# Output stage of a hybrid convolution/attention block on one core: VectorE's order pinned with the additions first, the convolution product's results written over its loaded operands, the last weight splits on GpSimd

## The chip, the cores and the metric

The kernel runs on one core of one Trainium2 chip. The core has five engines with instruction streams of their own: TensorE (PE, and PEld for its weight loads), VectorE (DVE), ScalarE (ACT), GpSimd (POOL) and SyncE (SP), which here issues nearly all DMA transfers. An engine works through its stream in order; where an instruction waits for another engine or for a transfer, all that stands behind it on that engine waits as well. The metric is the device time of one execution in microseconds; the time before is the median of three runs.

## What is computed

One decoder layer over a sequence of 2048 tokens with model width 1024, all in float32 (the reference, cut to the part that matters here):

```python
h = rms_norm(x, norm_w) * (1 + scale) + shift
a, b, g_conv, q, k, v, g_attn, m_conv, m_attn = split(h @ w_in)
...                                   # convolution branch -> u, attention branch -> o
y_conv = u @ w_conv_out               # (2048 x 1024) @ (1024 x 1024)
y_attn = o @ w_attn_out
y = sigmoid(m_conv) * y_conv + sigmoid(m_attn) * y_attn
out = y @ w_out
x = x + gate * out
```

The change lies in the last three lines: the product `u @ w_conv_out` with the merge behind it, and the output product `y @ w_out` with the residual addition.

## The kernel before

Every float32 operand of a matmul is split into a high part h (a copy to the reduced format fp32r, on ScalarE) and a low part l = source - h (a subtraction of 128x512 on VectorE or GpSimd), and a product is the sum of three matmuls per 128 rows: h·h, h·l, l·h. TensorE's order is the program's order (a manual schedule). The order on the other engines is chosen when the kernel is built, by the scheduler of the framework with a model of time, except for instructions handed to `tc.keep_in_program_order`, which stay in the program's order among themselves.

*The convolution product* (L1451 to L1484) has four token blocks t of 512 tokens and in each eight blocks dm of 128 output columns, "yc t_dm". Each takes 24 matmuls. For each, SP loads two 256 KB tiles: the gate `gt` (the trace calls it mc, L1474; pool `gp`, three buffers) and the finished attention part `ya` (the trace: yl, L1476; pool `ys`, tag "yt", four buffers). When the product is in PSUM, VectorE makes `yt = (gt + 1) * pz` (L1482) and `yt = yt + ya` (L1483), where `yt` is another tile of tag "yt", and SP stores it to the scratch array `y_d` in HBM (L1484). So a block takes two of the four buffers of "yt".

*The weights of the output product.* During the last token block (t = 3) `w_out` is loaded in four pieces, `wo_fetch` (L1367): `wo_raw0`, and `wo_raw1` to `wo_raw3` in pool `op` under the tag "raw" with four buffers. They are multiplied by the adaLN gate (`wo_scale`, L1375). GpSimd forms combinations in place (L1400), and `wo_split` (ScalarE L1390, then `eng` at L1391) splits them into the operands of the product: B11, B21, T1, T3, T2 during the last blocks, B22 and T4 (called through `wo_rest`, L1403) from the output stage's hooks. Each name has four pieces k = 0 to 3.

*The output stage* works in eight quads j, each of 2 x 128 tokens by 2 x 512 columns, with a Strassen-Winograd scheme of seven products instead of eight. The products are A11·B11, A12·B21, S2·T2, S1·T1, S3·T3, S4·B22, A22·T4 with the numbers 0 to 6, where A are quarters of y, S their combinations, B quarters of the scaled weights and T their combinations. They run in the order `WO_ORDER = (0, 3, 2, 1, 4, 5, 6)` of product() (L1498), which is called with product numbers 0, 3, 2, 1, 4, 5, 6 in the quad as well; each has 12 matmuls of 128x512 (L1504). There are three PSUM banks: pa (the trace: oa), pb (ob), pc (oc). The first, third, fifth and seventh product accumulate in pa one on the other, the fourth goes to pb, the second and sixth to pc. After every product VectorE adds the bank to an x tile (L1491); a product that goes on accumulating in a bank can start only when the addition of the bank's last state has read it.

For a quad, `y_load` (L1409) reads the quarters of y from `y_d` into a tile `yq{j}` (two transfers of 512 KB; tag "raw", the same four buffers as wo_raw1 to wo_raw3), `y_split` (L1416) forms one S where needed (GpSimd, L1422 to L1427, in place but for S1, "ys") and splits the operand (ScalarE yh L1431, VectorE yl L1432). The splits run five products ahead (`LEAD`). `x_load` (L1444) loads four x tiles per quad; for the even quads from 2 on, and two tiles of quad 0, they are of tag "yt". The results are stored at L1496. Note that the trace uses "yl" both for the loaded attention part (L1476) and for the low part of a y operand (L1432).

*The hooks* (`out_hooks`) place the rest: in quad 0, after the first two products, the B22 splits (L1536 and after; even k on VectorE, odd k on GpSimd), after the third to sixth the T4 splits (all on VectorE); in each quad after the first product the y load of the next quad, after the fourth its x loads, and after each product the y split five products on. A hook is called inside product(), so in the program it stands ahead of that product's addition.

Of the kernel before, what the change touches and what calls it, by code (L numbers as in the profile page):

```python
# [10 lines left out]
F32 = mybir.dt.float32  # L11
# [4 lines left out]
ALU = mybir.AluOpType  # L16
AX = mybir.AxisListType

P = 128
# [35 lines left out]
def tile_hybrid_block(  # L55
# [5 lines left out]
    nc = tc.nc  # L61
# [3 lines left out]
    def pool(name, bufs=1, **kw):  # L65
        return tc.tile_pool(name=name, bufs=bufs, reuse_waits="tile", **kw)
# [8 lines left out]
    def bank(tag, name):  # L75
        return psum.tile([P, 512], F32, tag=tag, name=name)
# [9 lines left out]
    y_d = dram.tile([KC, P, S], F32, name="y_d")  # L86
# [33 lines left out]
    with pool("start", side="right") as st:  # L120
# [34 lines left out]
        n = tab[:, :, 1, :]  # L155
# [340 lines left out]
    def merge_z(half, j, wts, hooks):  # L496
        pz = bank("z" if half == 0 and j < 4 else "zzss"[j % 4], f"pzg{half}_{j}")
        z_tokens(pz, 256, *wts, j, hooks)
        return pz
# [80 lines left out]
    def spread_load(load):  # L580
        box = []
        return {16: [lambda: box.append(load())], 23: [lambda: box.pop()()]}
# [118 lines left out]
    for i in range(8):  # L701
        half, k = divmod(i, 4)
# [22 lines left out]
    for g in GROUPS:  # L725
        for h in range(NH):
            u = NH * GROUPS.index(g) + h
            state = {}
            for j in range(NB):
# [14 lines left out]
                if u == 0 and j >= NB - 2:  # L744
                    rest = []
                    for i in range(4):
                        f = loads[4 * (j - NB + 2) + i]
# [19 lines left out]
                i = NB * (u - 2 * NH) + j - 2  # L767
# [19 lines left out]
    for j in range(3):  # L787
        hooks = {}
# [4 lines left out]
        pz = merge_z(0, j, cur, hooks)  # L793
# [50 lines left out]
    for step, (half, j) in enumerate(order):  # L844
# [11 lines left out]
        hooks = spread_load(loads[step - 4]) if 4 <= step < 4 + KC else {}  # L856
        while len(turns) >= 2:
            hooks.setdefault(3, []).append(turns.pop(0))
        pz = merge_z(half, j, wts[half], hooks)
# [302 lines left out]
    for at, (i, n) in enumerate(slots):  # L1162
# [23 lines left out]
        for name, k in asked[:2]:  # L1186
            own, tag = (gp, "gt") if k < 3 else (cv, "ld")
# [21 lines left out]
    def right(name):  # L1209
        c = tc.tile_pool(name=name, bufs=1, side="right", reuse_waits="tile")  # L1210
        return c, c.__enter__()
# [5 lines left out]
    ys = big["raw"] = ys_c.__enter__()  # L1217
# [82 lines left out]
    def at_block(n, m, f):  # L1300
        plan.setdefault(n, {}).setdefault(m, []).append(f)
# [33 lines left out]
    for t in range(NT):  # L1335
        tsl = slice(512 * t, 512 * t + 512)
        for dm in range(KC):
            gt = gp.tile([P, 512], F32, tag="gt", name=f"ma{t}_{dm}")
            nc.sync.dma_start(gt, ma_d[dm, :, tsl])
            pz = bank("zso"[dm % 3], f"ya{t}_{dm}")  # L1340
# [3 lines left out]
            yt = ys.tile([P, 512], F32, tag="yt", name=f"yt{t}_{dm}", bufs=4)  # L1344
# [14 lines left out]
    WO_ORDER = (0, 3, 2, 1, 4, 5, 6)  # L1359
# [26 lines left out]
    def wo_split(name, k, src, eng=nc.vector):  # L1386
        if name not in wo:
            wo[name] = wo_place(name)
        h, l = (x[k] if isinstance(x, list) else x[:, k] for x in wo[name])
        nc.scalar.activation(h, src, AF.Copy)  # L1390
        eng.tensor_tensor(l, src, h.bitcast(F32), op=ALU.subtract)  # L1391

    def wo_first(k):
        w = wo_raw[k]
# [8 lines left out]
    def wo_rest(name, k, eng=nc.vector):  # L1403
        h, c = {"T3": (0, 0), "T2": (0, 1), "T4": (1, 0), "B22": (1, 1)}[name]
        wo_split(name, k, wo_raw[k][:, h, c], eng)

    LEAD = 5
# [8 lines left out]
    def y_split(j, i):  # L1416
        a11, a12, a21, a22 = (ysrc[j][:, q].rearrange("p k t -> p (k t)") for q in range(4))
        pool_tt = nc.gpsimd.tensor_tensor
        n = WO_ORDER[i]
        if n == 0:  # L1420
            s1 = ysrc[j, "S1"] = ys.tile([P, 512], F32, tag="fraw", name=f"ys1_{j}", bufs=3)
            pool_tt(s1, a21, a22, op=ALU.add)  # L1422
            pool_tt(a21, a11, a21, op=ALU.subtract)
        if n == 2:
            pool_tt(a11, ysrc[j, "S1"], a11, op=ALU.subtract)
        if n == 4:
            pool_tt(a12, a12, a11, op=ALU.subtract)  # L1427
        src = (a11, a12, a11, ysrc[j, "S1"], a21, a12, a22)[n]
        own, tag, bufs = (op, "y", 2) if (j, i) in ((0, 0), (0, 1)) else (up[1], "u", KC)
        h, l = ya_of[j, n] = [own.tile([P, 512], F32R, tag=tag + hl, name=f"y{hl}{j}_{n}", bufs=bufs) for hl in "hl"]  # L1430
        nc.scalar.activation(h, src, AF.Copy)  # L1431
        nc.vector.tensor_tensor(l, src, h.bitcast(F32), op=ALU.subtract)  # L1432

    ysrc, ya_of, xin = {}, {}, {}

# [15 lines left out]
    for t in range(NT):  # L1451
        tsl = slice(512 * t, 512 * t + 512)
        if t == NT - 1:
            lnp_c.__exit__(None, None, None)
            wop_c, wop = right("wop")
            ap_c.__exit__(None, None, None)
            up_c[1].__exit__(None, None, None)
            op_c = pool("op", bufs=2)
            op = op_c.__enter__()
            for k in range(1, 4):  # L1460
                at_block(KC * t, 2, lambda k=k: wo_fetch(k))
                at_block(KC * t + (1, 2, 3)[k - 1], 1, lambda k=k: wo_scale(k))
            for k in range(4):
                at_block(KC * t + (0, 1, 2, 4)[k], (3, 6, 15, 3)[k], lambda k=k: wo_first(k))
            for i, (name, k) in enumerate((b, k) for b in ("T2", "T3") for k in range(4)):
                at_block(KC * t + 4 + i // 2, 4 + 11 * (i % 2), lambda name=name, k=k: wo_rest(name, k))
            at_block(KC * t + 4, 8, lambda: y_load(0))
            for i in range(2):
                at_block(KC * t + 6, 6 + 6 * i, lambda i=i: y_split(0, i))
            for q in (0, 3):  # L1470
                at_block(KC * t + 5, 8, lambda q=q: x_load(0, q))
        for dm in range(KC):
            gt = gp.tile([P, 512], F32, tag="gt", name=f"mc{t}_{dm}")
            nc.sync.dma_start(gt, mc_d[dm, :, tsl])  # L1474
            ya = ys.tile([P, 512], F32, tag="yt", name=f"yl{t}_{dm}", bufs=4)
            nc.sync.dma_start(ya, ya_d[dm, :, tsl])  # L1476
            pz = bank("zso"[dm % 3], f"yc{t}_{dm}")
            sl = slice(P * (dm % 4), P * (dm % 4) + P)
            project(pz, [h[:, sl] for h, _ in wc[dm // 4]], [l[:, sl] for _, l in wc[dm // 4]],
                    norms[t].uh, norms[t].ul, plan.get(KC * t + dm))  # L1480
            yt = ys.tile([P, 512], F32, tag="yt", name=f"yc{t}_{dm}", bufs=4)
            nc.vector.scalar_tensor_tensor(yt, gt, 1.0, pz, op0=ALU.add, op1=ALU.mult)  # L1482
            nc.vector.tensor_add(yt, yt, ya)  # L1483
            nc.sync.dma_start(y_d[dm, :, tsl], yt)  # L1484

    HB = NB // 2

    def out_quad(j, hooks):
        pa, pb, pc = bank("z", f"oa{j}"), bank("s", f"ob{j}"), bank("o", f"oc{j}")
        x11, x12, x21, x22 = (xin.pop((j, q)) for q in range(4))  # L1490
        add = lambda dst, ps: nc.vector.tensor_tensor(dst, dst, ps, op=ALU.add)  # L1491
        begun = set()

        def store(q, t):
            jj, c = j + HB * (q // 2), q % 2
            nc.sync.dma_start(out2[P * jj : P * jj + P, 512 * c : 512 * c + 512], t)  # L1496

        def product(n, ps, more=False):  # L1498
            yh, yl = ya_of.pop((j, n))
            wh, wl = ([x[k] if isinstance(x, list) else x[:, k] for k in range(4)] for x in wo[PRODUCTS[n][1]])  # L1500
            yh, yl = ([y[:, P * k : P * k + P] for k in range(4)] for y in (yh, yl))
            terms = [t for k in range(4) for t in ((yh[k], wh[k]), (yh[k], wl[k]), (yl[k], wh[k]))]
            for m, (y, w) in enumerate(terms):
                nc.tensor.matmul(ps, y, w, start=(m == 0 and ps.name not in begun), stop=(m == 11 and not more),  # L1504
                                 skip_group_check=True)
            begun.add(ps.name)
            hooks(WO_ORDER.index(n))

        product(0, pa, True)
        add(x11, pa)  # L1510
        product(3, pc, True)
        add(x22, pc)
        product(2, pa, True)
        add(x12, pa)
        product(1, pb)
        add(x11, pb)
        store(0, x11)
        product(4, pa, True)
        add(x22, pa)
        store(3, x22)  # L1520
        product(5, pc)
        add(x12, pc)
        store(1, x12)
        product(6, pa)
        add(x21, pa)
        store(2, x21)

    for q in (1, 2):
        x_load(0, q)
# [3 lines left out]
    def out_hooks(j):  # L1533
        def f(i):
            if j == 0 and i < 2:
                for k in (2 * i, 2 * i + 1):  # L1536
                    wo_rest("B22", k, (nc.vector, nc.gpsimd)[k % 2])
            elif j == 0 and i < 6:
                wo_rest("T4", i - 2)
            if j + 1 < HB and i == 0:  # L1540
                y_load(j + 1)
            if j + 1 < HB and i == 3:
                for q in range(4):
                    x_load(j + 1, q)
            at = 7 * j + i + LEAD
            if at < 7 * HB:
                y_split(at // 7, at % 7)
        return f
# [38 lines left out]
```

## Time and profile before

| | |
|---|---|
| median of 3 runs | 2425.87 us |
| lowest, highest run | 2423.82, 2425.93 us |
| the profiled execution: its own time | 2423.63 us |
| its span, first to last instruction | 2421.7 us |
| mean granted TensorE clock | 0.994 |
| first matmul of the output stage | 2249.9 us |
| last addition of the output stage | 2418.0 us |

All times inside the profile count from the span's start. A line of a timeline gives start and duration in us, the engine, the source line, the operation, the tiles written and read, their shapes and how many instructions were put together (x3); in brackets stands the engine's idle time before it and what ended that. A line of a view of waits gives who waited for whom, the total in us, how often, and the longest. "SPq" rows are transfers that SP issues; their duration is that of the issuing, not of the transfer.

### The profile page before, as it was taken

To read this page: it belongs to the slowest core of one execution; us is meant where nothing else is said; L and a number is where in the kernel's file an instruction comes from. 1 tells how busy PE (TensorE), PEld (TensorE's weight loads), DVE (VectorE), ACT (ScalarE), POOL (GpSimd) and SP (SyncE) were. 2 spreads that over 40 slices of the span, in tenths; PEclk is the share of its full clock that TensorE was granted. 3 is DMA by queue.
4 is the path that set the end of the run, shared out by engine and by line. 5 is a ranking of instruction groups with operands and counts; after the bars stand their busy time and mean duration, and the time that the engine had idled before them with its cause. 6 is when DMAs were issued, how large, how long until landed. Compare 5 with 4: busy or idle time off the path is not lost. (4 is left out here: it accounts for less than half of the span.)

```text
span 2421.7 us, 39474 instructions
## 1 busy us (share of the span) xinstructions
PE 2372.0 (98%) x12785; PEld 2117.9 (87%) x12785; DVE 1734.9 (72%) x3941; ACT 998.0 (41%) x2790; POOL 839.7 (35%) x949
## 2 busy tenths in 40 slices
PE   6999999999999999999999999999999999999899
PEld 2989999999999999999888888878888888888687
DVE  5865655555555565567779999989999977787643
ACT  4833433343343444344544444554444444431221
POOL 3421111111111111112467777775565620004420
PEclk8999999999999999999999999999999999999999
DMA  7633543454453222115664544674444469865742
GB/s 256 219 115 110 158 128 102 142 150 140 145 154 89 70 67 61 31 49 176 211 207 138 164 154 133 211 231 125 136 150 132 156 221 315 285 198 185 215 145 83
DMA packets 349468, 372.99 MB, mean 154 GB/s; under 512 B 29704, under 2 KB 251176, under 8 KB 349262
## 3 DMA queue, kind: packets, MB, share of 16 engines
q1 hardware_dynamic: 335966, 346.80, 46.1%
q10 hardware_dynamic: 13296, 23.66, 2.7%
q8 instruction: 102, 1.67, 0.3%
q14 instruction: 104, 0.85, 0.1%
HBM read 231.74 MB, written 138.61 MB: 153 GB/s over the span
## 5 line engine op out<-in xcount | busy, mean ns | idle before, releaser
L370 PE MATMUL pz<-wh_u,hT_lo 128*128 128x384 f32 x1536 | 537.1, 350 | 5.2 <-DVE hT_lo L289 3.8
L370 PE MATMUL pz<-wh_u,hT_hi 128*128 128x384 f32 x1536 | 518.3, 337 | 5.3 <-ACT wh_u L346 2.9
L370 PE MATMUL pz<-wl_u,hT_hi 128*128 128x384 f32 x1536 | 518.9, 338 | 0.6 <-DVE wl_u L349 0.6
L398 DVE SCALAR_TENSOR_TENSOR qk<-pz,st,wqk 128x128 f32<-128x128 f32 x384 | 117.0, 346 | 318.3 <-POOL st L114 318.1
L113 POOL TENSOR_SCALAR st<-st 128x2 f32<-128x2 f32 x192 | 47.3, 247 | 812.7 <-ACT sq L387 812.7
L370 PEld LDWEIGHTS pz<-wh_u,hT_hi 128*128 128x128 f32 x1536 | 290.7, 189 | 8.2 <-ACT wh_u L346 3.6
L370 PEld LDWEIGHTS pz<-wh_u,hT_lo 128*128 128x128 f32 x1536 | 289.4, 188 | 8.1 <-DVE hT_lo L289 4.6
L370 PEld LDWEIGHTS pz<-wl_u,hT_hi 128*128 128x128 f32 x1536 | 289.8, 189 | 2.0 <-DVE wl_u L349 1.5
L434 ACT ACTIVATE qkT<-ptq 128x256 f32<-128x256 f32 x192 | 73.6, 383 | 420.2 <-PE ptq L432 419.7
L1033 DVE SCALAR_TENSOR_TENSOR ce<-us,pair_taps,ce 128x512 f32<-128x512 f32 x240 | 179.8, 749 | 1.7
L1004 DVE SCALAR_TENSOR_TENSOR ce<-ut,chan,ce 128x512 f32<-128x512 f32 x240 | 179.5, 748 | 0.0
L1017 DVE SCALAR_TENSOR_TENSOR cq<-ut,chan,cq 128x512 f32<-128x512 f32 x208 | 156.5, 752 | 4.2
L919 POOL TENSOR_TENSOR slT<-wT,shT 128x512 fp32r<-128x512 f32 x97 | 129.4, 1336 | 75.3 <-ACT shT L918 75.3
L387 ACT ACTIVATE sq<-pz 128x128 bf16<-128x128 f32 x384 | 106.0, 276 | 99.6 <-PE pz L370 92.6
L114 POOL TENSOR_TENSOR st<-st,mhalf 128x2 f32<-128x2 f32 x192 | 136.6, 712 | 16.0
L918 ACT ACTIVATE shB<-wB 128x512 fp32r<-128x512 f32 x120 | 75.5, 631 | 152.0 <-issue 44.5
L918 ACT ACTIVATE shT<-wT 128x512 fp32r<-128x512 f32 x100 | 63.1, 631 | 153.0 <-issue 66.2
L919 POOL TENSOR_TENSOR slB<-wB,shB 128x512 fp32r<-128x512 f32 x77 | 102.4, 1330 | 68.5 <-ACT shB L918 67.1
L447 ACT ACTIVATE sm<-sm,osb 128x128 f32<-128x128 f32 (+1 forms) x192 | 88.7, 462 | 62.6 <-DVE osb L445 59.6
L461 PE MATMUL po<-lv,pT 128*128 128x128 f32 x600 | 97.2, 273 | 0.0
L461 PEld LDWEIGHTS po<-lv,pT 128*128 128x128 f32 x600 | 93.0, 189 | 0.5 <-issue 0.5
L445 DVE CUSTOM_DVE_ANT_0 sm<-ps,mask 128x128 f32<-128x128 f32 (+1 forms) x192 | 68.7, 358 | 26.5 <-PE ps L442 26.4
(666 smaller groups left out, 6331.5 us busy)
## 6 DMA issues: line engine op xcount, KB each, us to landing
wB<-in_w_in_dram SPq DMA_DIRECT2D x140, 256.0 KB, 3.3
qkv_d<-qkv SPq DMA_DIRECT2D x128, 192.0 KB, 2.2
wT<-tT_d SPq DMA_DIRECT2D x80, 256.0 KB, 2.7
raw_u<-in_w_in_dram SPq DMA_DIRECT2D x93, 192.0 KB, 2.8
lqk<-qkv_d SPq DMA_DIRECT2D x128, 128.0 KB, 2.3
tT_d<-wB ACTq DMA_DIRECT2D x60, 256.0 KB, 2.8
acc_d<-osb SPq DMA_DIRECT2D x192, 65.0 KB, 1.8
at<-acc_d SPq DMA_DIRECT2D x64, 195.0 KB, 3.5
```

What stands on the lines that cost most here:

```text
L114: nc.gpsimd.tensor_tensor(dst, scratch[:, :n], mhalf[:, :n], op=ALU.pow)
L370: nc.tensor.matmul(pz[:, :width], part(a, k, P * j, P), w[:, :width], start=(m == 0), stop=(m == 23))
L387: nc.scalar.activation(sq, pz[:, P * i : P * i + P], AF.Square, scale=1.0 / math.sqrt(P), accum_out=st[:, i : i + 1])
L398: nc.vector.scalar_tensor_tensor(qk[:, 2 * i : 2 * i + 2].rearrange("p a b -> p (a b)"), pz[:, P * i : P * i + P], st[:, 2 + i : 3 + i], w ...
L434: nc.scalar.activation(qkT.rearrange("p a b -> p (a b)"), pt[:, :256], AF.Copy)
L447: nc.scalar.activation(sm[:, :w], sm[:, :w], AF.Exp, scale=-1.0, bias=o[:, P : P + 1], accum_out=o[:, P + 1 : P + 2])
L461: nc.tensor.matmul(po[:, :P], box["pT"][:, P * i : P * i + P], vt, start=(i == 0), stop=(i == nk - 1))
L918: nc.scalar.activation(h, q[name], AF.Copy)
L919: eng.tensor_tensor(l, q[name], h.bitcast(F32), op=ALU.subtract)
L1004: stt(box["e"], e[:, 1 + j : 513 + j], chan[:, cb, 2 * j : 2 * j + 1], box["e"], op0=ALU.mult, op1=ALU.add)
L1017: stt(box["o"], o[:, 2 + j : 514 + j], w, psum_o, op0=ALU.mult, op1=ALU.add)
L1033: stt(dst, box["both"][:, 1 + j : 513 + j], pair_taps[:, cb, j : j + 1], box["e"], op0=ALU.mult, op1=ALU.subtract if j == 0 else ALU.add)
```

## The change

1. *Order pinned on VectorE.* Three kinds of instruction are kept in program order among themselves: the additions of the output stage, the y splits from quad 0's sixth product on, and the T4 splits on VectorE. And the hooks are called behind the addition of their product, not ahead of it.
2. *Results over the operands.* The convolution product's first VectorE operation writes over the gate tile, the second over the loaded attention part, which is then stored. A block so takes one buffer of "yt", not two, and the ya load of a block takes the buffer that the store of four blocks earlier has read. The gate tile comes free after the second operation instead of the first.
3. *Late splits on GpSimd.* All four B22 splits and the T4 splits k = 1 and 3 run on GpSimd; T4 k = 0 and 2 stay on VectorE. Four subtractions move in all.

```diff
@@ wo_split
-        eng.tensor_tensor(l, src, h.bitcast(F32), op=ALU.subtract)
+        ins = eng.tensor_tensor(l, src, h.bitcast(F32), op=ALU.subtract)
+        if name == "T4" and eng is nc.vector:
+            tc.keep_in_program_order(ins)
@@ y_split
-        nc.vector.tensor_tensor(l, src, h.bitcast(F32), op=ALU.subtract)
+        ins = nc.vector.tensor_tensor(l, src, h.bitcast(F32), op=ALU.subtract)
+        if (j, i) >= (0, LEAD):
+            tc.keep_in_program_order(ins)
@@ convolution product
-            yt = ys.tile([P, 512], F32, tag="yt", name=f"yc{t}_{dm}", bufs=4)
-            nc.vector.scalar_tensor_tensor(yt, gt, 1.0, pz, op0=ALU.add, op1=ALU.mult)
-            nc.vector.tensor_add(yt, yt, ya)
-            nc.sync.dma_start(y_d[dm, :, tsl], yt)
+            nc.vector.scalar_tensor_tensor(gt, gt, 1.0, pz, op0=ALU.add, op1=ALU.mult)
+            nc.vector.tensor_add(ya, ya, gt)
+            nc.sync.dma_start(y_d[dm, :, tsl], ya)
@@ out_quad
-        add = lambda dst, ps: nc.vector.tensor_tensor(dst, dst, ps, op=ALU.add)
+        add = lambda dst, ps: tc.keep_in_program_order(nc.vector.tensor_tensor(dst, dst, ps, op=ALU.add))
...
             begun.add(ps.name)
-            hooks(WO_ORDER.index(n))
 
         product(0, pa, True)
         add(x11, pa)
+        hooks(0)
         product(3, pc, True)
         add(x22, pc)
+        hooks(1)
...
         product(6, pa)
         add(x21, pa)
         store(2, x21)
+        hooks(6)
@@ out_hooks
             if j == 0 and i < 2:
                 for k in (2 * i, 2 * i + 1):
-                    wo_rest("B22", k, (nc.vector, nc.gpsimd)[k % 2])
+                    wo_rest("B22", k, nc.gpsimd)
             elif j == 0 and i < 6:
-                wo_rest("T4", i - 2)
+                wo_rest("T4", i - 2, (nc.vector, nc.gpsimd)[i % 2])
```

More of the change, by code (lines that the diff above doesn't have):

```diff
@@ L1506, in product @@
             begun.add(ps.name)
-            hooks(WO_ORDER.index(n))
         product(0, pa, True)
         add(x11, pa)
+        hooks(0)
         product(3, pc, True)
         add(x22, pc)
+        hooks(1)
         product(2, pa, True)
         add(x12, pa)
+        hooks(2)
         product(1, pb)
@@ L1517, in out_quad @@
         store(0, x11)
+        hooks(3)
         product(4, pa, True)
@@ L1520, in out_quad @@
         store(3, x22)
+        hooks(4)
         product(5, pc)
@@ L1523, in out_quad @@
         store(1, x12)
+        hooks(5)
         product(6, pa)
```

## The prediction

> **What bounds the kernel now.** I read the page first (busy shares), then TensorE's waits over the last 320 us, then the chain of waits and the engines' timelines around the one wait that is left there.
>
> ```profile
> span 2421.7 us, 39474 instructions
> PE 2372.0 (98%) x12785; PEld 2117.9 (87%) x12785; DVE 1734.9 (72%) x3941; ACT 998.0 (41%) x2790; POOL 839.7 (35%) x949
> ```
> ```profile
> PE oa L1504 <- DVE xt L1491: 8.9, 1, 8.9
> ```
> TensorE is busy 98% of the span, and in the stages that the change touches it waits for long once only: 8.9 us, for an addition of the first output quad. The chain that ended last shows where:
>
> ```profile
> 2261.99 1.81 DVE woloT L1391 x3
> 2263.79 0.61 DVE xt L1491
> 2264.40 0.14 issue
> 2264.53 5.21 PE oa L1504 x12
> 2269.74 2.81 PE ob L1504 x12
> 2272.55 2.80 PE oa L1504 x12
> 2275.35 2.80 PE oc L1504 x12
> 2278.15 5.60 PE oa L1504 x24
> ```
> ```profile
> 2249.90 0.40 PE L1504 MATMUL oa<-wohB,yh 128*128 128x512 f32 x1
> ```
> The first product of the quad starts at 2249.90 and a product takes 2.80, so the third is due at 2255.50. It accumulates in the bank of the first (pa) and starts at 2264.53, when the addition that reads that bank is done. It then takes 5.21 instead of 2.80. The seventh product starts at 2278.15; undisturbed it would at 2255.50 + 4 x 2.80 = 2266.7. The place costs 11.4 us (0.47%), which is all that the change can win here. Windows (columns: PE, PEld, DVE, ACT, POOL busy, granted clock, DMA share, GB/s) explain the 5.21:
>
> ```profile
> 2255.60:2259.10 3.50, 0.01 (x1) 0.00 (x0) 3.50 (x4) 2.19 (x5) 3.50 (x3) 1.00 0.55 153
> 2259.10:2264.50 5.40, 0.00 (x0) 0.00 (x0) 5.40 (x10) 1.04 (x3) 1.13 (x1) 0.50 0.29 80
> 2264.50:2269.30 4.80, 4.76 (x11) 3.80 (x12) 1.78 (x3) 1.00 (x2) 1.60 (x2) 0.50 1.12 335
> ```
> The clock falls to 0.50 some 3.5 us into the idle time and is still there for 4.8 us of work after it: 5.21 - 2.80 = 2.4 us. VectorE was busy all through the gap, with other things:
>
> ```profile
> 2250.90 0.69 DVE L1483 TENSOR_TENSOR yc<-yc,yl 128x512 f32<-128x512 f32 x1 [2.82 <-DMA yl<-ya_d]
> 2253.87 1.89 DVE L1432 TENSOR_TENSOR yl<-yq,yh 128x512 fp32r<-128x512 f32 x3
> 2255.68 3.43 DVE L1391 TENSOR_TENSOR woloB<-wo_raw,wohiB 128x512 fp32r<-128x512 f32 x2
> 2259.62 1.76 DVE L1432 TENSOR_TENSOR yl<-yq,yh 128x512 fp32r<-128x512 f32 x2
> 2261.91 1.88 DVE L1391 TENSOR_TENSOR woloT<-wo_raw,wohiT 128x512 fp32r<-128x512 f32 x3
> 2263.72 0.67 DVE L1491 TENSOR_TENSOR xt<-xt,oa 128x512 f32<-128x512 f32 x1
> ```
>
> **The additions first.** In the new built order the first addition follows the last convolution block's two operations directly; the two B22 splits (3.43), the three T4 splits (1.88) and two of the y splits (1.76) no longer stand ahead of it. What is then last is the load of the last block's gate operand, mc: by the sum below it issues about 2250.7, and the ya loads of the same size land 2.9 to 4.8 us after issue (second landing row below), which gives 2253.6 to 2255.5; two block operations and the addition, 0.69 + 0.69 + 0.67, and the 0.14 of the chain put the third product at 2255.8 to 2257.7, 0.3 to 2.2 us late, less than the 3.5 after which the clock fell. So the old stall goes.
>
> **What the pins put in its place.** After three additions and T4's first split, the pinned order on VectorE is: y split of quad 1 for its first product; addition of quad 0's fourth product (bank pb); y split of quad 1 for its second product; addition of quad 0's fifth product (bank pa). The seventh product writes pa and so waits for that last one. Both splits need yq1, quad 1's y. Before, those additions were not held by yq1. So the question is when yq1 is loaded, and there two of the other parts come in. (1) Its buffer: the rotation of four gives it wo_raw1's, whose last reader is now T4's split k=1 on GpSimd. (2) Its place in SP's queue: writing results over the loaded operands means that a ya load four blocks on, and four x loads, take a buffer that a store still reads, so each waits for a store's landing, and SP issues nothing meanwhile. In the new SP order come: store 3_3, mc, ya 3_7 (waits for store 3_3), store 3_4, mc 3_7, x (waits for 3_4), store 3_5, x (waits for 3_5), store 3_6, x (waits for 3_6), store 3_7, two x, x (waits for 3_7), x, and then yq1. Before, yq's next load stood right behind the first two x loads:
>
> ```profile
> 2246.01 0.32 SPq L1484 DMA_DIRECT2D y_d<-yc  x1
> 2253.98 0.32 SPq L1484 DMA_DIRECT2D y_d<-yc  x1
> 2254.35 2.61 SPq L1444 DMA_DIRECT2D xt<-in_x_dram  x2
> 2261.45 1.00 SPq L1413 DMA_DIRECT2D yq<-y_d  x2
> ```
> ```profile
> DMA to landing us min/median/max: 2.8/4.2/4.3
> ```
> ```profile
> DMA to landing us min/median/max: 2.9/4.7/4.8
> ```
> These two are the landings over 2140 to 2262 of the stores of y (L1484) and of the ya loads (L1476). Let W be the time from the issue of such a store to what waits for it. With store 3_3 at 2246.0 as before and 0.4 for an issue, the five serial waits give yq1 at 2248.9 + 5W. The second x load above waited for the store of 2253.98 until 2.65 us after it (2254.35 + 2.61 - 0.33); that store had no load close ahead of it. In the new order each store is issued right behind a load, as the ones that took 4.2 to 4.3. I take W = 3.8, nearer to the latter, since the x loads ahead of three of the five are the shorter ones: yq1 at 2267.9 (2262.2 with 2.65, 2270.4 with 4.3).
>
> GpSimd's bound on yq1 lies earlier:
>
> ```profile
> 2255.30 1.58 POOL L1427 TENSOR_TENSOR yq<-yq 128x512 f32<-128x512 f32 x1 [14.07 <-DVE yl L1432]
> 2256.84 3.39 POOL L1391 TENSOR_TENSOR woloB<-wo_raw,wohiB 128x512 fp32r<-128x512 f32 x2
> 2267.62 1.27 POOL L1422 TENSOR_TENSOR ys<-yq 128x512 f32<-128x512 f32 x1 [7.39 <-DMA yq<-y_d]
> ```
> ```profile
> 2268.93 0.63 ACT L1431 ACTIVATE yh<-ys 128x512 fp32r<-128x512 f32 x1 [2.34 <-POOL ys L1422]
> ```
> One combination, four B22 splits and T4 k=1, at 1.3 alone to 1.7 beside VectorE, from 2251.6 (the y splits move up with the earlier ya loads) or 2255.3 (as before): done between 2259.4 and 2265.5. This costs nothing as long as SP is later; without that cover it is 2259.4 to 2265.5 that decides. B22 itself is done by 2263.8 at worst and is used at 2263.9.
>
> From yq1's issue on, the rows of before give: 6.17 to GpSimd's sum ys (2261.45 to 2267.62), 1.31 to its yh (2268.93), 0.63, the split 0.68, the addition 0.67, 0.14: 9.6; I take 10.0, since that sum may take 1.7. The seventh product then starts at 2277.9 instead of 2278.15: -0.25. TensorE has by then idled 9 to 11 us once more (from 2266.7, or 0.3 to 2.2 later), so its clock falls again: +2.4, as measured above. Sum: -0.25 + 2.4 = +2.15 us.
>
> [...]
>
> **Edits at nothing.** Writing over gt and ya changes no duration on VectorE (0.69 each). A gate buffer comes free 0.7 us later; no yc product waits above, and blocks take 5.6. In the later quads TensorE has no gap and VectorE is half idle:
>
> ```profile
> 2283.80:2303.30 19.50, 19.50 (x85) 15.71 (x84) 10.48 (x14) 4.36 (x8) 9.33 (x7) 1.00 0.61 184
> ```
> There the pinned split stands five products (14 us) ahead of its use, against some 1.3 + 0.7 + 0.7 of work. T4 on GpSimd (k=1, 3) is done about 2269, before its product.
>
> [...]
>
> **Rivals.** *The stall is simply gone or short.* If store landings don't hold SP up (W under 2.4), GpSimd's early end decides: yq1 2259.4, seventh product 2269.4, 2.7 us late and with the clock up (it held for 3.5): 2269.4 - 2278.15 = -8.8, to 2417.1; with no stall at all 2414.4. For it: 2.65 was seen once. Against it: 4.2 is the median. With W = 2.65 the stall still costs the clock: 2272.2, -3.5.
>
> *SP's serial waits decide, longer.* One mechanism: five waits, each worth 1 us of the end per us of W. At W = 4.34 the loss passes 0.2%; at 4.8 (the longest ya landing) yq1 goes at 2272.9, the seventh product at 2282.9: +7.2, to 2433.0. For it: the median of 4.2 gives +4.2 already; more x loads are in flight than before. Against it: a store behind an x load had 2.65.
>
> *The change doesn't do what it says:* the third product still waits for over 3.5 us, mc 3_7 landing after 2256.8; its clock loss adds 2.4 to the sum, and the seventh waits as well: +4.6, at the edge of what can be told, to 2430.4. Against it: ya 3_7 and mc are issued 2 to 4 us before they are needed.
>
> **How the numbers follow.** The profiled execution took 2423.63 (span 2421.7 and 1.9 around it), 2.2 below the median 2425.87, near the lowest run; it becomes 2425.8. On the median: 2425.87 + 2.15 = 2428.0. A measurement here can tell 0.2%, 4.85 us, from no change. Forecast (the stall moves to the seventh product, W from 2.4 to 4.3): 0.42, its own range 2421.5 to 2430.5. Gone or short: 0.23. SP's waits longer: 0.29. Third product still late: 0.06, counted as slower. So faster 0.23, same 0.42, slower 0.35. The range leaves out the full gain and losses beyond W = 4.8: 2418 to 2433.
>
> **What would show it.** Right: no wait of TensorE at the third product over 3 us, a wait of 7 to 11 us at the seventh, on the addition behind the split of quad 1; SP's rows show x loads waiting for y_d stores, yq1 issued about 2268; clock 0.50 after the stall. Wrong: yq1 issued before 2262, GpSimd's split as what its load waits for, or TensorE waiting for B22 or T4.

## The result and the profile after

| | before | changed |
|---|---|---|
| median of 16 runs each | 2425.35 us | 2430.25 us |
| lowest to highest run | 2423.09 to 2428.11 | 2426.39 to 2433.93 |
| ratio to before, 95% interval | | 1.0022 (1.0014 to 1.0029) |
| the profiled execution, its span | 2423.63, 2421.7 | 2427.53, 2425.7 |

The changed kernel is slower by 4.9 us on the medians, 0.2%: right at the bound of what the prediction called a change. The two profiled executions differ by 3.9 us, 2.8 of them in the output stage. The old stall of 8.9 us is gone, and two others stand in its place. TensorE's waits in the late stages of the changed kernel:

```profile
PE oa L1507 <- DVE xt L1494: 6.5, 1, 6.5
PE oa L1507 <- ACT yh L1433: 4.0, 1, 4.0
```
The second of these is the third product. The profile names ScalarE, for this row of its timeline, which ends at 2260.78:

```profile
2259.63 1.15 ACT L1433 ACTIVATE yh<-yq 128x512 fp32r<-128x512 f32 x2 [9.04 <-POOL yq L1429]
```
But the third product reads none of the operands made there. What it waits for in the built order is the addition that ended 0.03 us earlier (2260.07 + 0.68), in VectorE's timeline:

```profile
2258.39 0.68 DVE L1485 SCALAR_TENSOR_TENSOR mc<-mc,yc 128x512 f32<-128x512 f32 x1
2259.10 1.04 DVE L1486 TENSOR_TENSOR yl<-yl,mc 128x512 f32<-128x512 f32 x1
2260.07 0.68 DVE L1494 TENSOR_TENSOR xt<-xt,oa 128x512 f32<-128x512 f32 x1
2260.67 1.16 DVE L1434 TENSOR_TENSOR yl<-yq,yh 128x512 fp32r<-128x512 f32 x1
...
2275.04 0.69 DVE L1434 TENSOR_TENSOR yl<-yq,yh 128x512 fp32r<-128x512 f32 x1 [8.48 <-ACT yh L1433]
2275.65 0.68 DVE L1494 TENSOR_TENSOR xt<-xt,ob 128x512 f32<-128x512 f32 x1
2278.15 1.20 DVE L1434 TENSOR_TENSOR yl<-ys,yh 128x512 fp32r<-128x512 f32 x1 [1.82 <-ACT yh L1433]
2279.27 0.67 DVE L1494 TENSOR_TENSOR xt<-xt,oa 128x512 f32<-128x512 f32 x1
```
The first addition follows the last block's two operations at once, as forecast, but late. The lower half is the new wait: VectorE stands idle 8.5 us ahead of the first y split of quad 1, then 1.8 ahead of the second, and the addition that the seventh product needs is behind both. SP's timeline says why these splits are late:

```profile
2250.68 0.32 SPq L1487 DMA_DIRECT2D y_d<-yl  x1
2251.05 0.42 SPq L1478 DMA_DIRECT2D mc<-mc_d  x1
2253.24 0.32 SPq L1480 DMA_DIRECT2D yl<-ya_d  x1
2253.65 0.38 SPq L1487 DMA_DIRECT2D y_d<-yl  x1
2254.08 0.43 SPq L1478 DMA_DIRECT2D mc<-mc_d  x1
2257.32 0.33 SPq L1448 DMA_DIRECT2D xt<-in_x_dram  x1
2257.75 0.38 SPq L1487 DMA_DIRECT2D y_d<-yl  x1
2261.01 0.33 SPq L1448 DMA_DIRECT2D xt<-in_x_dram  x1
2261.40 0.42 SPq L1487 DMA_DIRECT2D y_d<-yl  x1
2264.74 0.33 SPq L1448 DMA_DIRECT2D xt<-in_x_dram  x1
2265.16 0.38 SPq L1487 DMA_DIRECT2D y_d<-yl  x1
2265.64 3.61 SPq L1448 DMA_DIRECT2D xt<-in_x_dram  x4
2269.34 1.01 SPq L1415 DMA_DIRECT2D yq<-y_d  x2
```
Store, wait, load, four times over, at 3.3 to 3.7 us from a store to the x load that waits for its landing, and yq1 at the end. GpSimd, from which yq1's buffer must come free too, is done little earlier, and starts on yq1's sum 6.85 us after its issue:

```profile
2258.01 1.58 POOL L1429 TENSOR_TENSOR yq<-yq 128x512 f32<-128x512 f32 x1 [12.73 <-DVE yl L1434]
2259.56 6.36 POOL L1391 TENSOR_TENSOR woloB<-wo_raw,wohiB 128x512 fp32r<-128x512 f32 x4
2265.88 3.07 POOL L1391 TENSOR_TENSOR woloT<-wo_raw,wohiT 128x512 fp32r<-128x512 f32 x2
2276.19 1.26 POOL L1424 TENSOR_TENSOR ys<-yq 128x512 f32<-128x512 f32 x1 [7.24 <-DMA yq<-y_d]
```
The clock falls twice. In the windows of the changed kernel (columns as in the prediction) the granted clock is 0.61 and 0.53 behind the two stalls:

```profile
2261.00:2264.50 3.50, 3.50 (x10) 2.79 (x11) 2.52 (x3) 1.86 (x4) 3.50 (x3) 0.61 0.43 150
...
2280.20:2284.50 4.30, 4.30 (x11) 3.39 (x12) 4.05 (x4) 1.67 (x3) 4.10 (x4) 0.53 1.15 325
```

### The profile page after: what moved, and what is told of

It reads as the page before. It is cut to its first block, busy times and chain, and to the rows that moved or that the text cites. A ratio compares the mean times of both kernels' runs of the same rounds, so it can differ in the third digit from the quotient of the medians.

```text
span 2425.7 us, 39451 instructions
## 1 busy us (share of the span) xinstructions
PE 2374.1 (98%) x12785; PEld 2118.6 (87%) x12785; DVE 1733.3 (71%) x3937; ACT 996.3 (41%) x2790; POOL 847.7 (35%) x953
## 4 chain that ended last, share of the span: by engine, by line
PE 86%; DVE 3%; DMA 3%; POOL 2%; issue 2%; ACT 1%; SPq 0%; ACTq 0%; POOLq 0%; DVEq 0%
PE pz L370 31%; PE paab L955 7%; PE yc L1231 4%; PE ya L1231 4%; PE pag_g_d L955 4%; PE pag_mc_d L955 4%; PE pcab L955 3%; PE oa L1507 3%; PE pag_ma_d L955 3%; PE ps L442 3%; PE po L461 3%; PE pzg L370 3%; PE pcg_g_d L955 2%; PE pcg_mc_d L955 2%; PE ptq L432 2%; PE pbab L955 2%
```

## The experiments

An execution's part ahead of the output stage varies from one to the next (the output stage's first matmul stands at 2249.9 to 2255.9 us in the twelve profiles), so the profiles are compared from the first matmul of the output stage on. The table is worked out from the matmul rows of the traces: how much later than 2.80 us after its predecessor a product's first matmul starts (its wait), how much longer than 2.80 it is from there to the next product's first matmul (the low clock where a window is shown, in before, changed and E8; in E7 and E9 also a wait of 0.5 and 5.4 us inside the seventh product), the sum of all of this over the first 16 products, and the issue of yq1 after the first matmul. The ratios are those of the timed runs, each against runs of the kernel before taken in the same set; the medians of different rows come from different sets.

| kernel | third: wait | third: longer | seventh: wait | seventh: longer | lost, 16 products | yq1 issued at | median, us | ratio to before |
|---|---|---|---|---|---|---|---|---|
| before | 9.0 | 2.3 | 0 | 0 | 11.2 | 11.6 | 2425.35 | |
| changed | 4.1 | 1.4 | 6.6 | 2.0 | 14.0 | 18.2 | 2430.25 | 1.0022 |
| E1 without part 2 | 3.0 | 0.1 | 5.6 | 2.5 | 11.1 | 15.4 | 2427.35 | 1.0000 (0.9991 to 1.0009) |
| E2 without part 3 | 7.5 | 1.6 | 0 | 0 | 9.0 | 13.1 | 2426.39 | 1.0000 (0.9991 to 1.0009) |
| E3 part 2 alone | 9.9 | 1.9 | 0.5 | 0.1 | 12.3 | 13.6 | 2429.63 | 1.0009 (1.0001 to 1.0018) |
| E4 part 1 alone | 7.4 | 2.5 | 0 | 0 | 10.2 | 11.8 | 2424.65 | 0.9993 (0.9984 to 1.0001) |
| E5 quad 1's splits one hook later | 3.3 | 1.6 | 4.0 | 1.6 | 10.9 | 17.7 | 2428.30 | 0.9999 (0.9990 to 1.0008) |
| E6 x loads pinned | 4.3 | 1.6 | 3.0 | 1.4 | 10.4 | 14.9 | 2426.09 | 0.9996 (0.9987 to 1.0005) |
| E7 chain closed | 2.5 | 1.6 | 3.1 | 0.8 | 7.9 | 12.6 | 2424.64 | 0.9987 (0.9978 to 0.9995) |
| E8 E7, splits late | 2.4 | 1.6 | 0 | 0.2 | 4.5 | 12.5 | 2419.75 | 0.9967 (0.9956 to 0.9979) |
| E9 E8 with part 2 | 4.1 | 1.6 | 0 | 6.1 | 13.0 | 19.8 | 2428.55 | 1.0008 (0.9999 to 1.0017) |
| E10 E8, T3 late | 0 | 0 | 0 | 0 | 1.7 | 11.3 | 2417.17 | 0.9960 (0.9948 to 0.9973) |

Theory A, formed on the two traces: part 2's waits for store landings in SP's queue make both the last block's loads and yq1 late, and the pinned order hands yq1's lateness on to the seventh product; GpSimd's T4 split is a second bound on yq1, a little earlier. Its rivals are in the expectations.

### The parts one by one

**E1**, the changed kernel with part 2 undone:

```diff
-            nc.vector.scalar_tensor_tensor(gt, gt, 1.0, pz, op0=ALU.add, op1=ALU.mult)
-            nc.vector.tensor_add(ya, ya, gt)
-            nc.sync.dma_start(y_d[dm, :, tsl], ya)
+            yt = ys.tile([P, 512], F32, tag="yt", name=f"yc{t}_{dm}", bufs=4)
+            nc.vector.scalar_tensor_tensor(yt, gt, 1.0, pz, op0=ALU.add, op1=ALU.mult)
+            nc.vector.tensor_add(yt, yt, ya)
+            nc.sync.dma_start(y_d[dm, :, tsl], yt)
```


> The change without part 2 (separate result tiles again); pins and GpSimd splits stay. Theory A (SP's waits for store landings, which part 2 brings, make the last mc load and yq1 late): no x or ya load waits for a y_d store for more than 2 us, the third product waits at most 3 us, yq1 is issued about 2264 to 2265, bound by GpSimd's T4 split; some 3 to 5 us faster than the changed kernel, ratio to before 0.998 to 1.001. Theory B (the splits on GpSimd alone hold yq1, and part 2 costs nothing): the waits of the changed kernel, 4 us at the third and 6.5 at the seventh product, stay, and so does its time within 1.5 us, ratio 1.0015 to 1.003.

The third product waits 3.0 us, the seventh 5.6. In E1's timelines yq1 goes out in the very moment in which GpSimd's first T4 split is done (2268.12 + 1.27):

```profile
2261.32 6.85 POOL L1391 TENSOR_TENSOR woloB<-wo_raw,wohiB 128x512 fp32r<-128x512 f32 x4
2268.12 2.54 POOL L1391 TENSOR_TENSOR woloT<-wo_raw,wohiT 128x512 fp32r<-128x512 f32 x2
```
```profile
2262.30 3.54 SPq L1448 DMA_DIRECT2D xt<-in_x_dram  x5
2269.44 1.00 SPq L1415 DMA_DIRECT2D yq<-y_d  x2
```
As theory A had it, though yq1 went later than it had said (2264 to 2265 is at most 15.1 us after the first matmul, measured 15.4): without the landings GpSimd decides, 2.7 us earlier than SP did in the changed kernel. The seventh product gains little by that, 1.0 us of waiting, as the third is less late too and so the seventh is due earlier. Theory B is out, as the waits at both products shrank and the ratio fell by more than the two intervals leave to chance at their nearest ends (1.0009 against 1.0014).

**E2**, the changed kernel with part 3 undone:

```diff
-                    wo_rest("B22", k, nc.gpsimd)
+                    wo_rest("B22", k, (nc.vector, nc.gpsimd)[k % 2])
-                wo_rest("T4", i - 2, (nc.vector, nc.gpsimd)[i % 2])
+                wo_rest("T4", i - 2)
```


> The change without part 3 (B22 even pieces and all T4 pieces on VectorE again); pins and results over the operands stay. In its built order yq1 takes the buffer of yq0 and stands in SP's queue behind three store landings, not four, and two B22 splits and two y splits stand ahead of the first addition again. Theory A: yq1 about 2263 to 2266, no wait at the seventh product over 1 us, but a wait of 6 to 9 us at the third; ratio 0.998 to 1.001. Theory B: as there is no GpSimd split to wait for, the loss goes: ratio under 0.9985. Theory C (the pins themselves cost): the seventh product still waits over 3 us, ratio 1.0015 or more.

No wait at the seventh product, 7.5 at the third. Its SP timeline:

```profile
2262.81 0.42 SPq L1487 DMA_DIRECT2D y_d<-yl  x1
2266.15 0.33 SPq L1448 DMA_DIRECT2D xt<-in_x_dram  x1
2266.59 1.00 SPq L1415 DMA_DIRECT2D yq<-y_d  x2
```
Here yq1 follows directly on an x load that waited 3.3 us for a store: SP's landings decide, without GpSimd. So each of the two bounds holds yq1 by itself, to 13.1 us (SP, here) and 15.4 us (GpSimd, E1) where before had 11.6; the seventh product does not feel the 13.1, as the third is 7.5 us late. The 7.5 at the third product, more than the changed kernel's 4.1, show in VectorE's timeline of E2:

```profile
2259.49 3.43 DVE L1391 TENSOR_TENSOR woloB<-wo_raw,wohiB 128x512 fp32r<-128x512 f32 x2
2263.44 1.76 DVE L1434 TENSOR_TENSOR yl<-yq,yh 128x512 fp32r<-128x512 f32 x2
2265.73 0.68 DVE L1494 TENSOR_TENSOR xt<-xt,oa 128x512 f32<-128x512 f32 x1
```
Two y splits that are pinned run ahead of the pinned first addition, though the program has them behind it. So pinned instructions do not simply keep the program's order among themselves, as was said of `tc.keep_in_program_order` at the start. The rows fit another reading: a pin ties an instruction to the one traced just ahead of it on its engine, not to the last pinned one. With B22's even pieces on VectorE, unpinned, between the first addition and the y splits, the splits are tied to B22, B22 to nothing, and both float ahead of the first addition. Part 3 closed that chain by taking B22 off the engine; E7 tests the reading.

**E3**, the kernel before with part 2 alone (the first diff, reversed, on the kernel before):

> The kernel before with part 2 alone. Theory A: the store landings hold SP up here too: the stall at the third product stays at 9 us or grows by up to 2, yq1 is issued 2 to 4 us later than before and a second short wait of 1 to 4 us shows in the first two quads: 2 to 4 us slower than before, ratio 1.0008 to 1.002. Theory B: part 2 costs nothing: ratio 0.9995 to 1.0005.

The third product waits 0.9 us more than before, yq1 goes 2.1 us later; the second short wait is only 0.5 us, less than expected. The ratio stands for 2.2 us, of which the output stage of the profile shows 1.1 (12.3 against 11.2). TensorE's waits in the convolution stage of E3 have a row that the profile of before has not:

```profile
PE pc L1267 <- DVE red L1261: 1.3, 1, 1.3
```
E6 and E9, which have part 2 as well, show the same wait (0.6 and 0.9 us); the six kernels without it do not. The convolution stage takes 185.2 us from its first matmul to the output stage in all six profiles without part 2 (before, E1, E4, E7, E8, E10), and 185.2, 185.3, 186.8, 185.4, 186.0 and 186.3 in the six with it (changed, E2, E3, E5, E6, E9).

**E4**, the kernel before with part 1 alone (E1's and E2's edits together on the changed kernel):

> The kernel before with part 1 alone (pins, hooks behind the additions). The T4 splits no longer stand ahead of the first addition, the two B22 splits and two y splits still do. Theory A: the stall at the third product falls from 9 to about 7 us, none at the seventh; 1 to 2 us faster than before, ratio 0.999 to 0.9998. Theory C (the pins themselves cost): a stall of over 3 us at the seventh product too, ratio over 1.0005.

As expected: 7.4 at the third product, nothing at the seventh, a small gain that the interval does not set apart from none. The loss that theory C expected is not there. But this does not show that pins cost nothing: with the chain open and the third product this late, the seventh starts 27.1 us after the first matmul, behind anything that yq1 at 11.8 could hold up. E7 has the pins without this cover.

### What the seventh product waits for

**E5**, quad 1's y splits one hook later than in the changed kernel:

```diff
-            at = 7 * j + i + LEAD
-            if at < 7 * HB:
-                y_split(at // 7, at % 7)
+            for at in ((5,), (6,), (), (7,), (8,), (9, 10), (11,))[i] if j == 0 else (7 * j + i + LEAD,):
+                if at < 7 * HB:
+                    y_split(at // 7, at % 7)
```


> The changed kernel with quad 1's y splits one hook later: of the two only the one for its first product stands ahead of the fifth product's addition, the one that needs GpSimd's sum ys stands behind it. Theory A (the seventh product waits for yq1 through these splits): its wait shrinks by the way over GpSimd's sum, from 6.5 to 3 to 4.5 us, with yq1 issued as late as before (18 us after the first product's start); 2 to 3 us faster than the changed kernel, ratio to before 1.000 to 1.0015. Rival D (the seventh product waits for its own operand, T4 from GpSimd and from behind that addition): the wait stays within 1 us of 6.5, ratio 1.0015 to 1.003.

The wait falls from 6.6 to 4.0 us, with yq1 as late as before (17.7). That is the way over GpSimd's sum; with the rival D, T4 itself, the wait would have stayed. The ratio came out a hair better than expected.

**E6**, the changed kernel with the x loads of later quads held back on SP:

```diff
-        nc.sync.dma_start(t, x2[P * jj : P * jj + P, 512 * c : 512 * c + 512])
+        ins = nc.sync.dma_start(t, x2[P * jj : P * jj + P, 512 * c : 512 * c + 512])
+        if j > 1:
+            tc.keep_in_program_order(ins)
```


> The changed kernel with the x loads of quads 2 and later pinned behind what stands ahead of them in the program on SP, so that two waits for store landings no longer stand ahead of yq1; all else, the wait for GpSimd's T4 split too, stays. Theory A with both bounds: yq1 is issued 2 to 3 us earlier, at the end of GpSimd's T4 split k=1 (15 to 16.5 us after the first product's start, 18.2 in the changed kernel), the wait at the seventh product falls from 6.5 to 3.5 to 5 us, the one at the third stays near 4; ratio 1.000 to 1.0015. If SP's landings cost nothing (theory B): yq1 and the waits stay where they are, ratio 1.0015 to 1.003.

yq1 is issued 3.3 us earlier, again at the end of GpSimd's T4 split (2265.45 + 1.27 in E6's timeline, SP's row beside it):

```profile
2265.45 2.54 POOL L1391 TENSOR_TENSOR woloT<-wo_raw,wohiT 128x512 fp32r<-128x512 f32 x2
```
```profile
2263.72 1.72 SPq L1448 DMA_DIRECT2D xt<-in_x_dram  x3
2266.76 1.00 SPq L1415 DMA_DIRECT2D yq<-y_d  x2
```
The seventh product's wait falls by 3.6, from 6.6 to 3.0, a little more than expected, and the ratio is a little lower than expected; the third's wait stays. Theory A's price of SP's place in the queue, with part 2 and part 3 in: about 3.5 us.

### Versions with the chain of pins closed

**E7**: the kernel before, with part 1, and B22 on VectorE pinned too, so that the chain of pins has no gap:

```diff
-        if name == "T4" and eng is nc.vector:
+        if name in ("B22", "T4") and eng is nc.vector:
             tc.keep_in_program_order(ins)
```


> The kernel before with part 1, and the two B22 splits on VectorE pinned as well; no results over operands, no split moved to GpSimd. In the built order the first additions now stand ahead of B22, of the y splits and of T4, as in the changed kernel, and yq1 takes the buffer of yq0. Theory A: third product waits 2 to 3.5 us, yq1 about 12 to 13.5 us after the first product's start, so the seventh still waits 3 to 5 us; the clock may fall once: 2 to 4.5 us faster than before, ratio 0.998 to 0.9993. If the loss of the changed kernel lay in the pins (theory C): no gain, ratio over 0.9997.

2.5 and 3.1 us of waiting (and 0.5 inside the seventh product, for T4), where before had 9.0: the pins do what they were written for once nothing floats ahead of them. The 3.1 at the seventh product, with yq1 issued at 12.6, show what the pins can cost with neither part 2 nor part 3.

**E8**: E7, and the y splits of quad 1 behind the fifth product's addition:

```diff
-            at = 7 * j + i + LEAD
-            if at < 7 * HB:
-                y_split(at // 7, at % 7)
+            for at in ((5,), (6,), (), (), (7,), (8, 9), (10, 11))[i] if j == 0 else (7 * j + i + LEAD,):
+                if at < 7 * HB:
+                    y_split(at // 7, at % 7)
```


> As the run before, and the y splits of quad 1 only from behind the fifth product's addition on. Theory A: the third product waits 2 to 3.5 us, the seventh not at all (under 1 us), quad 1's first products under 2 us: 6 to 8.5 us faster than before, ratio 0.9965 to 0.9978. If theory A misses a bound, the stall of 4 us or more shows again at the first or second product of quad 1, ratio over 0.998.

0.9967: the seventh product no longer waits, and quad 1's own first products lose under 0.5 us.

**E9**: E8 with part 2 put back:

> The best kernel so far (pins with a closed chain, quad 1's splits behind the fifth addition, no split moved to GpSimd) with the results over the operands added. Theory A (part 2's store landings delay the last blocks and yq1): the third product waits 4 us or more, yq1 is issued 17 to 19 us after the first product's start instead of 12.5, and a wait of 3 to 5 us appears behind the seventh product, in quad 1; 5 to 8 us slower than the kernel without it, ratio to before 0.9988 to 1.0005. Theory B (part 2 costs nothing): ratio 0.996 to 0.9978.

8.8 us slower than E8 on the medians (of different sets), 0.41% by the ratios (8.5 us in the stage), more than expected, with yq1 at 19.8. The place differs from what was expected: the wait lies inside the seventh product, ahead of its last two matmuls, the first of which reads the low part of T4's piece k=3; in the pinned order that split stands behind quad 1's first. TensorE's waits in E9:

```profile
PE oa L1507 <- DVE woloT L1391: 5.4, 1, 5.4
PE oa L1507 <- ACT yh L1433: 4.0, 1, 4.0
```
Beside otherwise equal code this is the plainest price of part 2.

**E10**: E8 with T3's splits, which only the fifth product reads, moved from the last convolution blocks behind the first two additions:

```diff
-            for i, (name, k) in enumerate((b, k) for b in ("T2", "T3") for k in range(4)):
+            for i, (name, k) in enumerate((b, k) for b in ("T2",) for k in range(4)):
...
             if j == 0 and i < 2:
+                for k in (2 * i, 2 * i + 1):
+                    wo_rest("T3", k)
...
-        if name in ("B22", "T4") and eng is nc.vector:
+        if name in ("B22", "T4", "T3") and eng is nc.vector:
```


> The best kernel so far with T3's four splits taken out of the last convolution blocks and put, pinned, behind the first two additions; T3 is read by the fifth product only. If what is left of the third product's wait is VectorE's backlog, it falls from 2.4 to under 1.2 us and the clock stays up there (1.6 us more); 1.5 to 3.5 us faster than that kernel, ratio to before 0.9955 to 0.9968. If the loads of the last blocks (mc, ya) are what it waits for, the wait stays at 2 us or more and the ratio at 0.9965 to 0.998.

All that is left of TensorE's waits in the output stage of E10:

```profile
PE oa L1508 <- DVE xt L1495: 1.4, 2, 0.7
```
The third product starts on time, so its remaining 2.4 us in E8 came of the T3 splits in the last blocks: VectorE's backlog, or the ScalarE copies that moved with them, which this run does not separate. 2417.17 us, ratio 0.9960, 9.6 us below the kernel before in the same set. 1.7 of the 11.2 us are left.

## Why the prediction held, point by point

**The forecast as a whole.** The stall moves from the third product to the seventh and the time hardly changes, with a small loss: that is what happened, but for 4.1 us that stay at the third, and E5 and E6 show that yq1 through the pinned splits is the reason. Two of the signs named for being right were missed: no wait over 3 us at the third product (4.1), and 7 to 11 us at the seventh (6.6). The sum of +2.15 stands against +2.8 in the output stage of the profile (167.7 before, 170.4 changed, from its first matmul to its last) and +4.9 on the medians. Where the other 2.1 us of the medians come from stays open; part 2's longer convolution stage (E3) may be a share of it, but the changed kernel's own profile does not show it. That the median of 2430.25 still lies within the forecast's own range, by 0.25 us, is luck.

**The first addition follows the last block's operations.** Right in its order, wrong in its time: 0.3 to 2.2 us late was forecast, 4.1 measured, so the rival *third product still late*, given 0.06, came true as well. As a whole the trace is that rival's picture, a late third product and a late seventh, and its 2430.4 us is nearer to the measured 2430.25 than the forecast's 2428.0. The step that failed is "with store 3_3 at 2246.0 as before": it was issued at 2250.68, 3.4 us later when counted from the first product (2251.18, before 2249.90). The terms behind it were sound: from the issue of mc 3_7, measured at 2254.08, they give a third product at 2259.2 to 2261.1, and it started at 2260.89. Part 2's waits were counted from that store on, but they begin with the convolution stage. SP's waits there (2066 to 2200) are, before and changed:

```profile
SPq L1476 <- DMA y_d<-yc: 4.2, 2, 2.5
```
```profile
SPq L1480 <- DMA y_d<-yl: 58.4, 21, 4.5
```
Each ya load waits for a landing, and what stands behind it in SP's queue waits too. In sum SP hardly waits longer, though: all its waits in this stretch come to 88.7 us before and 89.5 changed, since before it waited 34.3 us for VectorE to free the gate buffers. The loads of `w_out` show what moved: the first of the last three goes out 45.3 us ahead of the output stage's first matmul instead of 46.8, and VectorE, on which the last blocks depend, waits for them and starts to scale the first 38.0 us ahead of it instead of 42.0. Its waits for them over 2090 to 2255, before and changed:

```profile
DVE wo_raw L1375 <- DMA wo_raw<-in_w_out_dram: 0.9, 1, 0.9
```
```profile
DVE wo_raw L1375 <- DMA wo_raw<-in_w_out_dram: 6.2, 2, 4.9
```
That this backlog is what carries the delay on to the third product is argued from the traces; E9 against E8 shows the whole price of part 2, not this way of it alone.

**W.** Taken as 3.8; measured 2.56 (2250.68 to 2253.24), 3.67, 3.26, 3.34, and about 3.3 for the last (the waiting load is the third of the four from 2265.64 on). The mean is 3.2: the four stores close behind loads took longer than the 2.65 seen before, less than the 4.2. The ground given for 3.8, that the x loads are the shorter ones, shows in their issuing alone (0.33 us in SP's timeline above, the mc loads 0.42 and 0.43); the landings of theirs that the profile before gives, over 2262 to 2300, took 5.2 us. The size was off by 0.6 each, 3 us in all, and store 3_3's delay made up for it: yq1 at 18.2 us after the first product, forecast 2267.9 - 2249.9 = 18.0. The right number came of two errors with opposite signs, by luck. Two slips in the working changed little: the rival on longer waits counts the 2.65 as a store behind an x load, where it was a store with no load close ahead and an x load behind it; and W = 2.4 gives 2421.0 us by the sum, not 2421.5.

**GpSimd's bound.** Forecast 2259.4 to 2265.5, measured 2267.4 (2265.88 and half of 3.07): later, as its start waits for a y split behind the same backlog. SP was still later, by 1.9 us. E1 and E6 show that GpSimd decides as soon as SP doesn't. So the cover that the prediction named was thin.

**From yq1 to the seventh product.** Forecast 10.0, measured 10.75 (2269.34 to 2280.09): GpSimd's sum began 6.85 after the issue, not 6.17, and the split beside it took 1.20, not 0.68.

**The clock.** +2.4 forecast, 2.0 measured behind the seventh product, and 1.4 behind the third, where none was forecast. "Less than the 3.5 after which the clock fell" was the wrong bound: in E8 2.3 us of idle time were followed by 3.41 us at half speed, and in E6 the seventh product was 3.0 us late and took 1.4 us longer (more in the last section).

**Edits at nothing.** In the later quads nothing changed, as forecast. "No yc product waits" holds, but another matmul of the convolution stage does in some executions (E3). The chain of pins was described wrongly: as an order among the pinned, which E2's rows contradict; they and E7 fit a tie to the neighbour.

**The rivals.** *Gone or short* needed W under 2.4; the smallest was 2.56. *SP's waits decide, longer* needed W of 4.34 or more: not seen, though the loss reached its mark by the other way. *The change doesn't do what it says* is what happened at the third product, and its sum came nearest to the measured time (above).

## What to carry to other kernels

Writing a result over its operand saved a buffer here and turned waits for an engine (34.3 us of SP's waits before) into waits for a store's landing (58.4 us): where those stand in the queue that issues nearly all loads, what is behind them can pay, far from the edit (8.5 us in the output stage, E9 against E8). Before instructions are pinned, ask of each what it waits for, since the pin hands its wait to all that follow (6.6 us at the seventh product of the changed kernel); and look in the built order for an unpinned neighbour that breaks the chain. When a stall is to be removed, work out what is late next (here yq1, then T3), and remove that in the same step: part 1 alone gave at most 0.16% by its interval, with the chain of pins closed and the next two bounds lifted it was 0.4%.

## What was unexpected of the hardware

The clock fell after less idle time than the 3.5 us that the first profile suggested. In E8 TensorE stood still for 2.3 us between the second and the third product, and the next matmuls ran at half speed for 3.4 us; in E1 it stood still for 2.9 us at the same place and went on at full speed. The matmul behind the gap, in E8 and then in E1:

```profile
2260.96 0.75 PE L1508 MATMUL oa<-wohiT,yh 128*128 128x512 f32 x1 [2.29 <-ACT yh L1433]
```
```profile
2262.64 0.48 PE L1508 MATMUL oa<-wohiT,yh 128*128 128x512 f32 x1 [2.93 <-ACT yh L1433]
```
The traces' record of the granted clock tells the two apart. In the profiles of before and changed it changes only on a grid of 3.41 us: the slow stretches behind the stalls last 10.24 us before (2259.08 to 2269.32), 3.41 and 6.83 changed (2260.34 to 2263.76, 2277.41 to 2284.24). Cut at the edges of such a grid, the windows (columns as in the prediction) show E8's whole gap in one window, with TensorE busy for 1.12 of 3.41 us, and the next window at half speed. In E1 the longer gap falls on two windows, with TensorE busy for 2.22 and 1.68 us, and the clock stays up:

```profile
2257.57:2260.98 3.41, 1.12 (x6) 0.62 (x4) 3.38 (x6) 1.28 (x3) 2.90 (x2) 1.00 0.61 187
2260.98:2264.39 3.41, 3.41 (x8) 2.73 (x9) 3.41 (x4) 1.95 (x4) 2.06 (x2) 0.50 0.87 257
```
```profile
2257.49:2260.90 3.41, 2.22 (x10) 1.50 (x8) 3.34 (x7) 0.00 (x0) 1.13 (x1) 1.00 0.73 208
2260.90:2264.32 3.42, 1.68 (x7) 1.43 (x8) 3.42 (x5) 2.93 (x6) 3.42 (x3) 1.00 0.64 193
2264.32:2267.73 3.41, 3.41 (x16) 2.73 (x15) 2.27 (x3) 0.30 (x1) 3.41 (x3) 1.00 0.92 277
```
Over the output stages of before and changed and in the windows above, no window at full speed with up to 51% of idle time (E1's second) was followed by half speed, and every one with 63% (changed, 2420.77 to 2424.18, TensorE busy for 1.25 of 3.41 us) or more was; what lies between, and what it takes for the clock to come back, these runs do not settle. For a forecast it means that a stall of 2.3 us can cost 1.6 us more, as in E8, and one of 2.9 us only 0.1, as in E1, by where it falls in the grid.
